# Halves of w_out and of two feed-forward units, made in the gate stage and fetched by DMA

## The chip, the cores and the metric

The kernel runs on one core of a Trainium2 chip. TensorE (PE) multiplies matrices; VectorE (DVE), ScalarE (ACT) and GpSimd (POOL) do elementwise work; SyncE (SP) issues DMA transfers, and ACT can issue them too, from its own instruction stream. The metric is the device time of one execution in microseconds (us). The two-letter names are those of the profile, where PEld is TensorE's weight load and SPq the DMA queue that SP issues to.

## The reference

One encoder layer on x of 1024 tokens by 1024 features, all in float32. Cut to what the kernel's stages around the change compute:

```python
q, k, v, r, lr_f, lr_b, u, g_a, g_b = split(rmsnorm(x) @ w_in)
o = gla(q, k, v, ...)                    # gated linear attention, both directions
y_a = (rmsnorm_head(o) * gla_norm * silu(r)) @ w_branch_gla
y_b = (multiscale_pool(u) @ w_pool_group) * pool_scale
merged = sigmoid(g_a) * y_a + sigmoid(g_b) * y_b
x = x + merged @ w_out
gate, up = split(rmsnorm(x) @ w_ffn_in)  # D_FF = 2816 each
x = x + (silu(gate) * up) @ w_ffn_out
return rmsnorm(x)
```

## The kernel before, in words

**Split operands.** Every float32 operand of a matmul is held as two parts in a narrower matmul type: hi is a cast on ACT (L172), lo is the operand less hi, a subtraction on DVE or POOL (L173). `products` (L250) makes three matmuls of them: hi by hi, hi by lo, lo by hi. The large products `o @ w_branch_gla`, `merged @ w_out` and the feed-forward ones are done with seven block products in place of eight (Strassen-like), so their operands are sums and differences of 512 x 512 blocks, numbered p = 1 to 7.

**Stages** (times by the profile's span): attention until some 405 us; the gate stage, 405 to 629; the branch product, 629 to 708; the out product with w_out, 708 to 813; the first feed-forward units, 813 to 900; the other units, and then the feed-forward output.

**The gate stage** is the loop `for g in range(GROUPS)`, with two feature blocks j for each g, so j runs from 0 to 7. Per j two weights `wa` and `wb` are multiplied (48 matmuls each, in two PSUM banks `ps`), and ACT evicts each bank with a sigmoid into `sa` (L899) and `sb` (L908). `take()` hands out a weight and begins the next, whose raw tiles SP loads (L180). `later` collects a store, and `flush` issues all that are collected, on SP (L686), at two places per j: behind the two halves of `wa` and behind those of `wb`. `weight_sums` runs beside this for j < 4, for w_branch_gla (two halves c of the rows) and then for w_out: it loads four raw blocks (`wsum`), POOL makes four sums or differences of 128 x 1024 in place (L750), and `later` stores them to `s_out` and `wt_out` in HBM. From j = 4 on, `beside` calls begin the data sums of the branch product.

**The branch and out products** share `project`: 14 pieces each (seven p, two halves c), 24 matmuls per piece. A piece needs data (`data_split`: ACT and DVE) and a weight (`weight_load` on SP into `wraw`, then `weight_split`: per half of 128 x 512 an ACT cast to `wh` and a POOL subtraction to `wl`). `line` lists the pieces; `line_make` makes the piece two ahead of the one that PE runs. The pool `wts` holds six buffers of `wh` and six of `wl`, shared with all other weights.

**Feed-forward units.** A `Unit` is one block of 128 gate and 128 up columns: two raw loads of 512 KB (`fraw`), up to four sums on DVE (`fs`, L1035), and seven `step`s, each with an ACT cast and a POOL subtraction of 128 x 512. Between the out product and the units, POOL makes the norm's scale (`n3rs`, L1150), DVE scales x to `xn` (L286), PE transposes `xn` (L1095) and ACT evicts it into `hb` (L1098), from which data halves `gh` and `gl` are split.

Tile's scheduler orders each engine's instructions; each engine runs its own list in order and waits on semaphores.

Of the kernel before, what the change touches and what calls it, by code (L numbers as in the profile page):

```python
# [3 lines left out]

# [6 lines left out]
F32 = mybir.dt.float32  # L11
# [6 lines left out]
P = 128  # L18
# [31 lines left out]
def kernel(  # L50
# [38 lines left out]
    def name(s):  # L89
        count[0] += 1  # L90
        return f"{s}_{count[0]}"

    def slot(dtype=F32, shape=(2, HALF), s="slot"):
        return slots.tile([P, *shape], dtype, tag="slot", name=name(s))
# [13 lines left out]
    def as_f32(ap):  # L108
        return ap.bitcast(F32)
# [61 lines left out]
    def split_to(hi, lo, src, eng=nc.vector):  # L171
        nc.scalar.copy(hi, src)  # L172
        eng.tensor_tensor(lo, src, as_f32(hi), op=ALU.subtract)  # L173
# [13 lines left out]
    class Weights:  # L187


        def __init__(self, tiles):  # L190
            self.per = tiles[0].shape[1]
            self.parts = []
            self.todo = [partial(self.split, raw) for raw in tiles]
            pending.extend(self.todo)
# [484 lines left out]
    deferred = []  # L679

    def later(dst, src):
        deferred.append(partial(nc.sync.dma_start, dst, src))

    def flush():
        while deferred:
# [42 lines left out]
    padd = partial(nc.gpsimd.tensor_tensor, op=ALU.add)  # L728


    s_out = {p: dram.tile([P, 4, HALF], F32, name=f"s_out{p}") for p in (3, 5, 6, 7)}
    wt_out = {p: dram.tile([P, 4, HALF], F32, name=f"wt_out{p}") for p in (4, 5, 6, 7)}

    def chunk(w, k_half, c_half, c):
        k0 = (4 * k_half + 2 * c) * P
        return w[k0 : k0 + 2 * P, c_half * HALF : (c_half + 1) * HALF].rearrange("(k p) c -> p k c", p=P)

    def weight_sums(w, c, left):
        raw = {}
        for i in range(2):  # L740
            for j in range(2):
                raw[i, j] = slot(s="wsum")
                nc.sync.dma_start(raw[i, j][:, :, :], chunk(w, j, i, c) if left else chunk(w, i, j, c))
        x11, x12, x21, x22 = (raw[i, j][:, :, :] for i in range(2) for j in range(2))
        if left:
            todo = [(padd, x22, x21, x22, 5), (psub, x21, x11, x21, 7), (psub, x11, x22, x11, 6), (psub, x12, x12, x11, 3)]
        else:
            todo = [(psub, x11, x12, x11, 5), (psub, x12, x22, x12, 7), (psub, x22, x22, x11, 6), (psub, x21, x21, x22, 4)]
        for op, dst, a, b, p in todo:
            op(dst, a, b)  # L750
            yield
            later((s_out if left else wt_out)[p][:, 2 * c : 2 * c + 2, :], dst)


    line, loads, made, begun_sums = [], [], [], []
# [18 lines left out]
    def weight_load(src):  # L774
        raw = slot(s="wraw")
        nc.sync.dma_start(raw[:, :, :], src)
        return raw

    def weight_split(raw):
        parts = []  # L780
        for k in range(2):
            hi = wts.tile([P, HALF], F32R, tag="wh", name=name("wh"))
            lo = wts.tile([P, HALF], F32R, tag="wl", name=name("wl"))
            split_to(hi[:, :], lo[:, :], raw[:, k, :], nc.gpsimd)
            parts.append((hi[:, :], lo[:, :]))
        return parts

    def data_split(src):
        hi, lo = slot(F32R, s="dh"), slot(F32R, s="dl")
        split_to(hi[:, :, :], lo[:, :, :], src[:, :, :])  # L790
        return [(hi[:, k, :], lo[:, k, :]) for k in range(2)]
# [39 lines left out]


    MERGED = (1, 7, 6, 5, 4, 2, 3)
    WEIGHT_B = {1: (0, 0), 2: (1, 0), 3: (1, 1)}
    merged = {}
    s3s = []

    def merged_piece(p, c):
        def load():
            if p in WEIGHT_B:  # L840
                return weight_load(chunk(w_out, *WEIGHT_B[p], c))
            return weight_load(wt_out[p][:, 2 * c : 2 * c + 2, :])

        def sums():
            def block(i, j):
                return merged[i, j][c][:, :, :]

            if p == 7:
                s3s.append(slot(s="s3"))
                sub(s3s[c][:, :, :], block(0, 0), block(1, 0))  # L850
            elif p == 6:
                padd(block(1, 0), block(1, 0), block(1, 1))
                sub(block(0, 0), block(1, 0), block(0, 0))
            elif p == 3:
                sub(block(0, 1), block(0, 1), block(0, 0))

        def make(raw):
            a = s3s[c] if p == 7 else merged[{1: (0, 0), 6: (0, 0), 5: (1, 0), 4: (1, 1), 2: (0, 1), 3: (0, 1)}[p]][c]
            return data_split(a), weight_split(raw)

        return load, sums, make

    line += [merged_piece(p, c) for p in MERGED for c in range(2)]

    sums_todo = [(w, c, left) for w, left in ((w_branch, True), (w_out, False)) for c in range(2)]
    summing = None
    def begin_first(c):
        begun[1, c] = data_split(ob[0, 0][c])

# [1 line left out]
    early += [partial(branch_sum, p, c) for p in (5, 7, 6) for c in range(2)]  # L871

    def beside(j):
        if j < 4:
            next(summing, None)
        elif early:
            early.pop(0)()

    for g in range(GROUPS):
        w = take()  # L880
        u = [t2(HALF + 2 * PAD, s="u") for _ in range(2)]
        nc.gpsimd.memset(u[0][:, :PAD], 0.0)
        nc.gpsimd.memset(u[1][:, PAD + HALF :], 0.0)
        for half in range(2):
            ps = feature_major(w, hT, half)
            nc.scalar.copy(u[half][:, PAD : PAD + HALF], ps[:, :])
        pool = slot(F32R, s="ph"), slot(F32R, s="pl")
        begin(pooled(g, u, *pool), 1)
        for j in (2 * g, 2 * g + 1):
            c = slice((j % 2) * P, (j % 2 + 1) * P)  # L890
            wa = take()
            if j == 2 * g:
                wp = take()(0)
            sa = slot(s="sa")
            if j < 4:
                summing = weight_sums(*sums_todo[j])
            for half in range(2):
                ps = feature_major(wa, hT, half)
                nc.scalar.activation(sa[:, half, :], ps[:, :], AF.Sigmoid)  # L899
                beside(j)  # L900
            flush()
            later(sa_out[:, :, j, :], sa[:, :, :])
            finish_side()
            wb = take()
            sb = slot(s="sb")
            for half in range(2):
                ps = feature_major(wb, hT, half)
                nc.scalar.activation(sb[:, half, :], ps[:, :], AF.Sigmoid)  # L908
                yb = bank(ps_g, "yb")
                mm3(yb[:, :], tuple(t[:, c] for t in wp), tuple(t[:, half, :] for t in pool), True, True)  # L910
                nc.vector.scalar_tensor_tensor(
                    sb[:, half, :], yb[:, :], g_pool[:, j : j + 1], sb[:, half, :], op0=ALU.mult, op1=ALU.mult
                )
                beside(j)
                if j == KT - 1 and half == 0:
                    line_make()
            if j < 4:
                next(summing, None)
            flush()
            later(yb_out[:, :, j, :], sb[:, :, :])  # L920
            if j == 3:
                for _ in range(3):
                    line_load()
            if j == KT - 1:
                line_make()
# [92 lines left out]
    class Unit:  # L1018
# [19 lines left out]
        def step(self, p=None):  # L1038

            if p is None:  # L1040
                if not self.todo:
                    return
                p = self.todo[0]
            self.todo.remove(p)
            if p in (5, 6) and not hasattr(self, "s1"):
                self.s1 = self.combined(self.block(1, 0), self.block(1, 1), ALU.add)
            if p == 1:
                src = self.block(0, 0)
            elif p == 6:
# [12 lines left out]
            lo = wts.tile([P, 4, P], F32R, tag="wl", name=name("wl"))[:, :, :]  # L1062
            split_to(hi, lo, src, nc.gpsimd)
            self.parts[p] = hi, lo
# [1 line left out]
        def __call__(self, p, k):  # L1066
            return tuple(t[:, k, :] for t in self.parts[p])

    f_order = [f for q in range(PAIRS) for f in (q, q + PAIRS)]
    units = []  # L1070

    def next_unit():
        if len(units) < FT:
            units.append(Unit(f_order[len(units)]))


    blocks, split_b, split_done = {}, {}, set()
# [470 lines left out]
```

## Time and profile before

| | |
|---|---|
| runs, median (lowest to highest of 3) | 1486.3 us (1485.8 to 1490.08) |
| profiled execution: time, span | 1487.58 us, 1485.8 us |
| mean granted clock of PE | 0.987 |
| instructions | 18520 |
| HBM read, written | 143.54 MB, 56.89 MB |

The profile shows one execution. It lists busy time per engine, the span in 40 slices, DMA queues, the chain that ended last, and the costliest groups of instructions: `out<-in`, shape, count, then busy time and mean length in ns, then the idle time ahead of them and what ended it. Other views answer for a stretch of the span: busy time by stage with the granted clock and DMA share, waits of an engine by the line and operation that released it, and the timeline.

### The profile page before, as it was taken

Reading aid. Unit: us, or ns where it says so; the run is one execution under the profiler, and the core shown is the slowest. Engines: PE = TensorE matmul, PEld = TensorE weight load, DVE = VectorE, ACT = ScalarE, POOL = GpSimd, SP = SyncE. Lnnn points to the kernel's source line nnn. Section 1 sums busy time; section 2 is a strip of 40 time slices with the busy share of each in tenths; the row PEclk is TensorE's granted clock in tenths of the full one; section 3 lists DMA queues with packets and bytes.
Section 4 is the critical chain, followed back from the end, with each engine's and each line's share of the span. In section 5 each row is a group of like instructions: output and inputs, shape, how many; then the busy total and the mean of one; then the engine's idle time right before and its main releaser. Section 6 shows DMA issues by size and latency. Waiting matters only on the chain. (4 is left out here: it accounts for less than half of the span.)

```text
span 1485.8 us, 18520 instructions
## 1 busy us (share of the span) xinstructions
PE 1419.6 (96%) x6797; PEld 1185.7 (80%) x6797; DVE 851.4 (57%) x1091; ACT 563.8 (38%) x1009; POOL 801.2 (54%) x544
## 2 busy tenths in 40 slices
PE   7999999999999999999888889999999999999988
PEld 7889898888888778878676667888888888787876
DVE  6175766761124053157783776677677777465375
ACT  6265555642122132244246533222333333443243
POOL 3241322312256432277897657667766668598345
PEclk9999999999999999999999989999999999999999
DMA  5120201001256732187242026444544456877352
GB/s 181 43 57 3 55 15 43 22 22 43 89 193 222 244 114 75 63 310 249 100 126 87 29 70 198 161 154 155 163 156 153 159 163 231 315 268 255 128 227 85
DMA packets 150523, 201.64 MB, mean 136 GB/s; under 512 B 9208, under 2 KB 96288, under 8 KB 150432
## 3 DMA queue, kind: packets, MB, share of 16 engines
q1 hardware_dynamic: 150432, 200.46, 40.4%
q8 instruction: 53, 0.87, 0.2%
q14 instruction: 38, 0.31, 0.1%
HBM read 143.54 MB, written 56.89 MB: 135 GB/s over the span
## 5 line engine op out<-in xcount | busy, mean ns | idle before, releaser
L173 POOL TENSOR_TENSOR wl<-raw,wh 128x512 fp32r<-128x512 f32 (+1 forms) x91 | 125.6, 1398 | 293.3 <-ACT wh L172 251.7
L250 PE MATMUL ps<-gh,wl 128*128 128x512 f32 x616 | 242.6, 394 | 9.4 <-POOL wl L173 9.4
L250 PE MATMUL ps<-gh,wh 128*128 128x512 f32 x616 | 243.0, 394 | 1.4 <-ACT wh L172 1.4
L250 PE MATMUL ps<-gl,wh 128*128 128x512 f32 x616 | 242.0, 393 | 0.0
L250 PE MATMUL ps<-hh,wh 128*128 128x512 f32 x576 | 228.5, 397 | 3.5 <-ACT wh L172 3.5
L250 PE MATMUL ps<-hh,wl 128*128 128x512 f32 x576 | 225.2, 391 | 0.6 <-POOL wl L173 0.6
L250 PE MATMUL ps<-hl,wh 128*128 128x512 f32 x576 | 225.0, 391 | 0.0
L173 POOL TENSOR_TENSOR wl<-fs,wh 128x512 fp32r<-128x512 f32 x88 | 127.7, 1453 | 107.0 <-ACT wh L172 75.8
L250 PEld LDWEIGHTS ps<-gh,wl 128*128 128x128 f32 x616 | 117.3, 190 | 35.7 <-POOL wl L173 11.0
L172 ACT CAST wh<-fs 128x512 fp32r<-128x512 f32 x88 | 54.6, 621 | 237.7 <-DVE fs L1035 237.7
L250 PEld LDWEIGHTS ps<-gh,wh 128*128 128x128 f32 x616 | 117.1, 190 | 26.0 <-ACT wh L172 2.3
L250 PEld LDWEIGHTS ps<-gl,wh 128*128 128x128 f32 x616 | 117.0, 190 | 24.0
L173 POOL TENSOR_TENSOR ol<-gor,oh 128x1024 fp32r<-128x1024 f32 (+1 forms) x42 | 108.8, 2607 | 47.6 <-ACT oh L172 35.2
L250 PEld LDWEIGHTS ps<-hh,wh 128*128 128x128 f32 x576 | 108.5, 188 | 25.1 <-ACT wh L172 3.9
L250 PEld LDWEIGHTS ps<-hh,wl 128*128 128x128 f32 x576 | 108.5, 188 | 24.2 <-POOL wl L173 1.1
L250 PEld LDWEIGHTS ps<-hl,wh 128*128 128x128 f32 x576 | 108.7, 189 | 21.0
L250 PE MATMUL ps<-oh,ol 128*128 128x512 f32 x308 | 120.2, 390 | 5.2 <-POOL ol L173 5.2
L250 PE MATMUL ps<-ol,oh 128*128 128x512 f32 x308 | 120.0, 390 | 2.9 <-DVE ol L173 2.9
L250 PE MATMUL ps<-oh,oh 128*128 128x512 f32 x308 | 120.0, 389 | 0.0
L173 POOL TENSOR_TENSOR wl<-wraw,wh 128x512 fp32r<-128x512 f32 x56 | 92.5, 1679 | 36.7 <-ACT wh L172 36.0
L173 DVE TENSOR_TENSOR ol<-wor,oh 128x1024 fp32r<-128x1024 f32 (+1 forms) x42 | 86.0, 2074 | 41.1 <-ACT oh L172 32.3
L173 POOL TENSOR_TENSOR wl<-fraw,wh 128x512 fp32r<-128x512 f32 x66 | 100.5, 1525 | 15.2 <-ACT wh L172 15.2
(246 smaller groups left out, 2894.7 us busy)
## 6 DMA issues: line engine op xcount, KB each, us to landing
raw<-in_w_in_dram SPq DMA_DIRECT2D x88, 256.0 KB, 3.3
fraw<-in_w_ffn_in_dram SPq DMA_DIRECT2D x44, 512.0 KB, 5.7
gor<-g_out SPq DMA_DIRECT2D x35, 512.0 KB, 5.2
g_out<-s SPq DMA_DIRECT2D x44, 256.0 KB, 2.4
wor<-t_out SPq DMA_DIRECT2D x20, 512.0 KB, 8.1
g_out<-g SPq DMA_DIRECT2D x33, 256.0 KB, 3.5
x<-in_x_dram SPq DMA_DIRECT2D x16, 512.0 KB, 4.4
wor<-in_w_ffn_out_dram SPq DMA_DIRECT2D x15, 512.0 KB, 7.5
```

The source lines that it names most:

```text
L172: nc.scalar.copy(hi, src)
L173: eng.tensor_tensor(lo, src, as_f32(hi), op=ALU.subtract)
L250: nc.tensor.matmul(ps, a[i], b[j], start=first and n == 0, stop=last and n == 2)
```

## The change

Four edits:

1. `later` issues its stores on ACT (`nc.scalar.dma_start`), all of them: `sa_out`, `yb_out`, `s_out`, and later `x2_out`.
2. For w_out, `output_parts` takes the place of `weight_sums`: all seven operands are made and split in the gate stage (hi on ACT, lo on DVE, 128 x 1024; the combinations stay on POOL), and both halves are stored to `wo_out`: 28 stores of 512 KB, where 8 sums were stored. In the out stage each piece fetches its four halves of 256 KB on SP straight into `wh` and `wl`; raw loads, casts and subtractions of these 14 pieces are gone.
3. `unit_parts` does the same for the first READY = 2 units: two loads, four combinations on POOL (128 x 512), seven casts on ACT, seven subtractions on DVE, seven stores of 512 KB each. A `ReadyUnit` step is two fetches of 256 KB.
4. Preparation is a chain of generators stepped four times per j through all eight j, so the early branch sums and `begin_first` move to j = 7 (two per step), and the first three loads of branch pieces from j = 3 to j = 6.

```diff
     def later(dst, src):
-        deferred.append(partial(nc.sync.dma_start, dst, src))
+        deferred.append(partial(nc.scalar.dma_start, dst, src))
...
+    def output_parts(c):
...
+        def parts(p, src):
+            hi, lo = slot(F32R, s="wph"), slot(F32R, s="wpl")
+            split_to(hi[:, :, :], lo[:, :, :], src)
+            for n, t in enumerate((hi, lo)):
+                later(wo_out[p][n][:, 2 * c : 2 * c + 2, :], as_f32(t[:, :, :]))
+
+        for p, src, dst, a, b in (
+            (1, b11, b11, b12, b11), (3, b22, b12, b22, b12), (7, b12, b22, b22, b11), (2, b21, b21, b21, b22)
+        ):
+            parts(p, src)
+            psub(dst, a, b)
+            if p in (3, 2):
+                yield
+        for p, src in ((5, b11), (6, b22), (4, b21)):
+            parts(p, src)
+            if p != 5:
+                yield
+        yield
+
+    def unit_parts(n):
...
+        def parts(p, src):
+            both = slot(F32R, s="up")
+            split_to(both[:, 0, :], both[:, 1, :], src)
+            later(u_out[n][p][:, :, :], as_f32(both[:, :, :]))
...
+        def weights():
+            parts = []
+            for k in range(2 * c, 2 * c + 2):
+                hi = wts.tile([P, HALF], F32R, tag="wh", name=name("wh"))
+                lo = wts.tile([P, HALF], F32R, tag="wl", name=name("wl"))
+                for n, t in enumerate((hi, lo)):
+                    nc.sync.dma_start(as_f32(t[:, :]), wo_out[p][n][:, k, :])
...
-            return data_split(a), weight_split(raw)
+            w = weights()
+            return data_split(a), w
...
+    preps = [g for c in range(2) for g in (branch_sums(c),)] + [output_parts(c) for c in range(2)]
+    preps = chain(*preps, *(unit_parts(n) for n in range(READY)))
...
     def beside(j):
-        if j < 4:
-            next(summing, None)
-        elif early:
-            early.pop(0)()
+        next(preps, None)
+        if j == KT - 1:
+            for _ in range(2):
+                early.pop(0)()
...
-            if j == 3:
+            if j == 6:
                 for _ in range(3):
                     line_load()
...
+    class ReadyUnit(Unit):
+        def step(self, p=None):
...
+            for i, t in enumerate((hi, lo)):
+                nc.sync.dma_start(as_f32(t), u_out[self.n][p][:, i, :].rearrange("p (k c) -> p k c", k=4))
```

The order of the matmuls on PE is the same. The other engines' lists change at these places. In the rows, the number behind a name is a counter; `wo_out_3987` to `wo_out_3993` are p = 1 to 7.

SP before, in the gate stage at j = 2 and 3: the stores of the sums stand between the loads of raw weights.

```order
L686 DMA yb_out<-sb_4319 256x1x512
L686 DMA wt_out_3988<-wsum_4529 128x1024
L180 DMA raw_4567<-in_w_in_dram 128x4x128
L180 DMA raw_4569<-in_w_in_dram 128x4x128
L686 DMA sa_out<-sa_4476 256x1x512
L686 DMA wt_out_3990<-wsum_4531 128x1024
L686 DMA wt_out_3989<-wsum_4535 128x1024
L686 DMA wt_out_3987<-wsum_4533 128x1024
L180 DMA raw_4648<-in_w_in_dram 128x4x128
L180 DMA raw_4650<-in_w_in_dram 128x4x128
```

ACT at the same place after: nine stores stand between the sigmoid of the second bank and the casts of the next weight; before, ACT went from the sigmoid straight to those casts.

```order
L172 CAST wph_4644<-wsum_4550 128x1024
L976 ACTIVATE sb_4599<-ps_4649 128x512
L172 CAST wph_4680<-wsum_4546 128x1024
L172 CAST wph_4684<-wsum_4552 128x1024
L686 DMA sa_out<-sa_4493 256x1x512
L686 DMA wo_out_3993<-wph_4639 128x1024
L686 DMA wo_out_3993<-wpl_4640 128x1024
L686 DMA wo_out_3988<-wph_4644 128x1024
...
L686 DMA wo_out_3992<-wpl_4685 128x1024
L172 CAST wh_4709<-raw_4697 128x512
L172 CAST wh_4719<-raw_4699 128x512
L967 ACTIVATE sa_4701<-ps_4702 128x512
```

POOL in the out stage before: the weights' low halves stand between the sums of merged blocks (L852) and the adds into x (L1179).

```order
L173 TENSOR_TENSOR wl_6356<-wraw_6309,wh_6355 128x512
L173 TENSOR_TENSOR wl_6360<-wraw_6309,wh_6359 128x512
L852 TENSOR_TENSOR mg_6046<-mg_6046,mg_6149 128x1024
L173 TENSOR_TENSOR wl_6408<-wraw_6349,wh_6407 128x512
L173 TENSOR_TENSOR wl_6412<-wraw_6349,wh_6411 128x512
L852 TENSOR_TENSOR mg_6047<-mg_6047,mg_6150 128x1024
L173 TENSOR_TENSOR wl_6448<-wraw_6401,wh_6447 128x512
L173 TENSOR_TENSOR wl_6452<-wraw_6401,wh_6451 128x512
```

After, POOL has there only the sums (L920), the adds (L1260, L1265) and the norm's scale (L1231), which now follows the adds directly.

```order
L920 TENSOR_TENSOR mg_6211<-mg_6211,mg_6312 128x1024
L920 TENSOR_TENSOR mg_6212<-mg_6212,mg_6313 128x1024
L1260 TENSOR_TENSOR x_1190_6348<-x_1190_6348,sum_6462 128x512
...
L1265 TENSOR_TENSOR x_1170_6249<-x_1170_6249,sum_6461 128x512
L1231 TENSOR_TENSOR n3rs_6893<-n3rs_6893,half_neg 128x1
L1231 TENSOR_TENSOR n3rs_6908<-n3rs_6908,half_neg 128x1
```

In its place SP has the fetches, four per piece, ahead of the out product:

```order
L1071 DMA x_1193_6354<-in_x_dram 128x1024
L908 DMA wh_6360<-wo_out_3987 128x512
L908 DMA wl_6361<-wo_out_3987 128x512
L908 DMA wh_6364<-wo_out_3987 128x512
L908 DMA wl_6365<-wo_out_3987 128x512
L908 DMA wh_6396<-wo_out_3987 128x512
```

More of the change, by code (lines that the diff above doesn't have):

```diff
@@ L2 @@
 from functools import partial
-from itertools import cycle
+from itertools import chain, cycle
 import concourse.bass as bass
@@ L731 @@
     s_out = {p: dram.tile([P, 4, HALF], F32, name=f"s_out{p}") for p in (3, 5, 6, 7)}
-    wt_out = {p: dram.tile([P, 4, HALF], F32, name=f"wt_out{p}") for p in (4, 5, 6, 7)}
+    wo_out = {p: dram.tile([2, P, 4, HALF], F32, name=f"wo_out{p}") for p in range(1, 8)}
+    READY = 2
+    f_order = [f for q in range(PAIRS) for f in (q, q + PAIRS)]
+    u_out = [{p: dram.tile([P, 2, HALF], F32, name=f"u_out{n}_{p}") for p in range(1, 8)} for n in range(READY)]
     def chunk(w, k_half, c_half, c):
@@ L736, in chunk, with branch_sums @@
         return w[k0 : k0 + 2 * P, c_half * HALF : (c_half + 1) * HALF].rearrange("(k p) c -> p k c", p=P)
-    def weight_sums(w, c, left):
+    def branch_sums(c):
         raw = {}
@@ L742, in weight_sums @@
                 raw[i, j] = slot(s="wsum")
-                nc.sync.dma_start(raw[i, j][:, :, :], chunk(w, j, i, c) if left else chunk(w, i, j, c))
+                nc.sync.dma_start(raw[i, j][:, :, :], chunk(w_branch, j, i, c))
+        yield
         x11, x12, x21, x22 = (raw[i, j][:, :, :] for i in range(2) for j in range(2))
[L745 to L748, printed above, removed]
@@ L749, in weight_sums @@
-        for op, dst, a, b, p in todo:
-            op(dst, a, b)
-            yield
-            later((s_out if left else wt_out)[p][:, 2 * c : 2 * c + 2, :], dst)
+        for op, dst, a, b, p in (
+            (padd, x22, x21, x22, 5), (psub, x21, x11, x21, 7), (psub, x11, x22, x11, 6), (psub, x12, x12, x11, 3)
+        ):
+            op(dst, a, b)
+            later(s_out[p][:, 2 * c : 2 * c + 2, :], dst)
+            if p in (7, 3):
+                yield
+        yield
+    def output_parts(c):
+        raw = {}
+        for i in range(2):
+            for j in range(2):
+                raw[i, j] = slot(s="wsum")
+                nc.sync.dma_start(raw[i, j][:, :, :], chunk(w_out, i, j, c))
+        yield
+        b11, b12, b21, b22 = (raw[i, j][:, :, :] for i in range(2) for j in range(2))
+        def parts(p, src):
[5 more added lines that the diff above has]
+            (1, b11, b11, b12, b11), (3, b22, b12, b22, b12), (7, b12, b22, b22, b11), (2, b21, b21, b21, b22)
+        ):
+            parts(p, src)
+            psub(dst, a, b)
+            if p in (3, 2):
+                yield
+        for p, src in ((5, b11), (6, b22), (4, b21)):
+            parts(p, src)
+            if p != 5:
+                yield
+        yield
@@ new lines, in unit_parts @@
+    def unit_parts(n):
+        raw = []
+        for c0 in (f_order[n] * P, D_FF + f_order[n] * P):
+            raw.append(slot(F32, (KT, P), "fraw"))
+            nc.sync.dma_start(raw[-1][:, :, :], w_ffn_in[:, c0 : c0 + P].rearrange("(k p) c -> p k c", p=P))
+        yield
+        a11, a12, a21, a22 = (t[:, 4 * j : 4 * j + 4, :].rearrange("p k c -> p (k c)") for t in raw for j in range(2))
+        def parts(p, src):
+            both = slot(F32R, s="up")
+            split_to(both[:, 0, :], both[:, 1, :], src)
+            later(u_out[n][p][:, :, :], as_f32(both[:, :, :]))
+        parts(1, a11)
+        parts(4, a22)
+        padd(a22, a21, a22)
+        psub(a21, a11, a21)
+        yield
+        parts(2, a12)
+        parts(5, a22)
+        psub(a11, a22, a11)
+        psub(a12, a12, a11)
+        yield
+        for p, src in ((7, a21), (6, a11), (3, a12)):
+            parts(p, src)
+        yield
+        yield
@@ L833 @@
     MERGED = (1, 7, 6, 5, 4, 2, 3)
-    WEIGHT_B = {1: (0, 0), 2: (1, 0), 3: (1, 1)}
     merged = {}
@@ L839, in load @@
         def load():
-            if p in WEIGHT_B:
-                return weight_load(chunk(w_out, *WEIGHT_B[p], c))
-            return weight_load(wt_out[p][:, 2 * c : 2 * c + 2, :])
+            return None
+        def weights():
[5 more added lines that the diff above has]
+                    nc.sync.dma_start(as_f32(t[:, :]), wo_out[p][n][:, k, :])
+                parts.append((hi[:, :], lo[:, :]))
+            return parts
         def sums():
@@ L858, in make @@
             a = s3s[c] if p == 7 else merged[{1: (0, 0), 6: (0, 0), 5: (1, 0), 4: (1, 1), 2: (0, 1), 3: (0, 1)}[p]][c]
-            return data_split(a), weight_split(raw)
+            w = weights()
+            return data_split(a), w
         return load, sums, make
     line += [merged_piece(p, c) for p in MERGED for c in range(2)]
-    sums_todo = [(w, c, left) for w, left in ((w_branch, True), (w_out, False)) for c in range(2)]
-    summing = None
+    preps = [g for c in range(2) for g in (branch_sums(c),)] + [output_parts(c) for c in range(2)]
+    preps = chain(*preps, *(unit_parts(n) for n in range(READY)))
     def begin_first(c):
@@ L894 @@
             sa = slot(s="sa")
-            if j < 4:
-                summing = weight_sums(*sums_todo[j])
             for half in range(2):
@@ L916 @@
                     line_make()
-            if j < 4:
-                next(summing, None)
             flush()
             later(yb_out[:, :, j, :], sb[:, :, :])
-            if j == 3:
+            if j == 6:
                 for _ in range(3):
@@ L1067, in __call__, with __init__ @@
             return tuple(t[:, k, :] for t in self.parts[p])
-    f_order = [f for q in range(PAIRS) for f in (q, q + PAIRS)]
+    class ReadyUnit(Unit):
+        def __init__(self, n):
+            self.n, self.parts, self.todo = n, {}, list(ORDER)
+        def step(self, p=None):
+            p = p or self.todo[0]
+            self.todo.remove(p)
+            hi = wts.tile([P, 4, P], F32R, tag="wh", name=name("wh"))[:, :, :]
+            lo = wts.tile([P, 4, P], F32R, tag="wl", name=name("wl"))[:, :, :]
+            for i, t in enumerate((hi, lo)):
+                nc.sync.dma_start(as_f32(t), u_out[self.n][p][:, i, :].rearrange("p (k c) -> p k c", k=4))
+            self.parts[p] = hi, lo
     units = []
@@ L1073, in next_unit @@
         if len(units) < FT:
-            units.append(Unit(f_order[len(units)]))
+            n = len(units)
+            units.append(ReadyUnit(n) if n < READY else Unit(f_order[n]))
     blocks, split_b, split_done = {}, {}, set()
```

## The prediction

> **What bounds the kernel now.** I read the page first, for the engine that fills the span.
>
> ```profile
> PE 1419.6 (96%) x6797; PEld 1185.7 (80%) x6797; DVE 851.4 (57%) x1091; ACT 563.8 (38%) x1009; POOL 801.2 (54%) x544
> PE   7999999999999999999888889999999999999988
> ```
>
> TensorE (PE) is busy for 96% of the span, and slices 20 to 24 of 40 (some 740 to 930 us) are the one dip after the start. The change leaves the list of matmuls alone, so it can only win PE's idle time and its time at a low clock. The second view gives busy time by stage: the stretch; its length, then PE, PEld, DVE, ACT, POOL; PE's granted clock, DMA share and GB/s.
>
> ```profile
> 461.00:517.00 56.00, 56.00 (x249) 46.39 (x248) 15.98 (x16) 11.75 (x22) 33.51 (x21) 1.00 0.70 231
> 517.00:573.00 56.00, 51.86 (x221) 42.13 (x220) 23.84 (x26) 15.48 (x27) 16.59 (x14) 0.97 0.41 122
> 400.00:629.00 229.00, 224.86 (x984) 185.44 (x983) 68.76 (x76) 52.67 (x94) 97.28 (x64) 0.99 0.48 154
> 629.00:708.00 79.00, 76.77 (x335) 62.27 (x334) 53.91 (x51) 32.45 (x48) 57.25 (x38) 1.00 0.73 266
> 708.00:813.00 105.00, 90.67 (x369) 69.12 (x368) 71.61 (x76) 47.31 (x84) 91.85 (x54) 0.93 0.33 108
> 813.00:900.00 87.00, 72.05 (x297) 57.00 (x296) 64.15 (x67) 35.23 (x54) 52.75 (x33) 0.90 0.23 76
> 900.00:1000.00 100.00, 100.00 (x442) 82.52 (x441) 67.97 (x77) 29.74 (x52) 72.72 (x51) 1.00 0.48 158
> ```
>
> In this order: the four-weight part of the gate stage in which sums of weights are made, what follows it, the whole gate stage, the branch products, the out stage, the first feed-forward units, and the steady state. The gate stage has room on every engine. The out stage has POOL at 91.85 of 105 us, and PE idle for 14.33 us; the first units have 14.95 us idle. The clock there is 0.93 and 0.90: (1 - 0.93) x 105 = 7.4 us and (1 - 0.90) x 87 = 8.7 us more. Lost in both: 29.3 + 16.1 = 45.4 us. From 900 on nothing is lost at first, so most of what can be won lies here. The third view, PE's waits (total, times, longest), out stage first, then first units:
>
> ```profile
> PE ps L250 <- POOL wl L173: 8.8, 9, 2.9
> PE ps L250 <- ACT hb L1098: 1.8, 2, 1.6
> PE tr L1095 <- DVE xn L286: 1.3, 1, 1.3
> PE ps L250 <- ACT wh L172: 0.4, 1, 0.4
> ...
> PE ps L250 <- POOL wl L173: 9.4, 3, 3.9
> PE tr L1095 <- DVE xn L286: 2.2, 1, 2.2
> PE tr L1095 <- ACT hb L1098: 1.8, 1, 1.8
> PE ps L250 <- ACT wh L172: 1.4, 1, 1.4
> ```
>
> Of 29.3 us idle, 8.8 + 0.4 + 9.4 + 1.4 = 20.0 wait for a half of a weight, nearly all for the low half that POOL subtracts. That low clocks follow such waits is in the timeline (start, length, idle before):
>
> ```profile
> 777.43 0.39 PE L250 MATMUL ps<-wh,dl 128*128 128x512 f32 x1
> 777.66 0.39 PE L250 MATMUL ps<-wh,dh 128*128 128x512 f32 x1
> 779.89 0.50 PE L250 MATMUL ps<-wl,dh 128*128 128x512 f32 x1 [1.84 <-POOL wl L173]
> 782.57 0.63 PE L250 MATMUL ps<-wl,dh 128*128 128x512 f32 x1
> 783.00 0.63 PE L250 MATMUL ps<-wh,dl 128*128 128x512 f32 x1
> 898.04 0.50 PE L250 MATMUL ps<-gh,wl 128*128 128x512 f32 x1 [2.96 <-POOL wl L173]
> ...
> 779.90:784.00 4.10, 4.10 (x10) 2.89 (x11) 0.00 (x0) 0.83 (x4) 4.10 (x4) 0.58 0.40 161
> 868.40:872.40 4.00, 3.94 (x9) 3.17 (x10) 4.00 (x5) 1.24 (x2) 4.00 (x4) 0.50 0.59 172
> 898.00:902.00 4.00, 3.96 (x16) 3.03 (x17) 0.54 (x1) 1.11 (x2) 4.00 (x3) 1.00 0.70 214
> ```
>
> Matmuls start 0.23 us apart before the wait of 1.84 us and 0.43 apart after it, at a clock of 0.58 for 4.1 us; the longest wait, of 3.9, is followed by 0.50; one of 2.96 by no drop. So a wait of 2 to 4 us costs its length again, mostly, and I let the clock loss go with the waits.
>
> **The change, out stage and first units.** Removed from POOL: 28 subtractions for w_out, half of the first row, and 14 for two units.
>
> ```profile
> L173 POOL TENSOR_TENSOR wl<-wraw,wh 128x512 fp32r<-128x512 f32 x56 | 92.5, 1679 | 36.7 <-ACT wh L172 36.0
> 778.57 4.97 POOL L173 TENSOR_TENSOR wl<-wraw,wh 128x512 fp32r<-128x512 f32 x4
> 784.09 0.76 DVE L286 TENSOR_SCALAR xn<-x,n3rs 128x1024 f32<-128x1024 f32 x1 [4.34 <-POOL n3rs L1150]
> L173 POOL TENSOR_TENSOR wl<-fraw,wh 128x512 fp32r<-128x512 f32 x66 | 100.5, 1525 | 15.2 <-ACT wh L172 15.2
> L172 ACT CAST wh<-fs 128x512 fp32r<-128x512 f32 x88 | 54.6, 621 | 237.7 <-DVE fs L1035 237.7
> ```
>
> That is 28 x 1.68 = 47 us of POOL's work for the out stage and 14 x 1.53 = 21 for the units; from ACT 42 x 0.62 = 26 us of casts; DVE loses its 8 sums for the units, some 10 us (128x512, taken at 1.25 us, between half and the whole of the 1.63 that a 128x1024 subtraction takes in a row below). The weight waits go: 20.0 less the 2.96 at 898, which stands at a unit beyond the two, gives 17. The third row shows who else stood behind POOL: four subtractions in a row until 783.5, then n3rs (the norm's scale), then DVE's xn, then PE's transposes. Of 1.3 + 2.2 us for xn I take 3 away, of 1.8 + 1.8 for hb (ACT, with fewer casts in its queue) 2. With the waits 22 of 29.3 us idle go, and of the 16.1 us at low clock the share of the longer waits, some 13. Together -35.
>
> What is late next: PE's wish for data that DVE splits (dl, gl). DVE has 136 of 192 us busy in these stages, less some 10 for the sums gone, in a time that shrinks to 159: 0.79, with adds into the merge and the residual that come in bursts. And the fetches: 56 + 28 of 256 KB on SP, issued two pieces ahead, into buffers that PE frees only one piece before. A piece is 24 matmuls of 0.227 = 5.4 us, so they have 5 to 10 us.
>
> ```profile
> raw<-in_w_in_dram SPq DMA_DIRECT2D x88, 256.0 KB, 3.3
> wraw<-s_out SPq DMA_DIRECT2D x8, 512.0 KB, 8.5
> ```
>
> The same size lands in 3.3 us where DMA is half free, and 512 KB in 8.5 us in the branch stage at a share of 0.73. Four of them are 1 MB per piece: 193 GB/s, below the 266 that the branch stage carried. Mostly in time; I give back 2 for fetches and DVE. Out stage and units: -33; with half of it back under other names -18; with all 45.4 gone but the 2.96 at 898 and half of hb's waits -40. I stay nearer the second, since the waits named POOL are the most of the row.
>
> **The gate stage.** Here two bad things before: PE waited once for 3.5 us, and its clock cost 0.03 x 56 = 1.7.
>
> ```profile
> 522.66 0.50 PE L250 MATMUL ps<-hh,wh 128*128 128x512 f32 x1 [3.52 <-ACT wh L172]
> 509.36 2.79 SPq L686 DMA_DIRECT2D wt_out<-wsum  x2
> 514.13 1.62 SPq L180 DMA_DIRECT2D raw<-in_w_in_dram  x2
> ```
>
> SP's stores of the sums wait for POOL, and the next raw weights stand behind them on SP. On ACT's queue the stores no longer hold a load: -5.8 (4.14 idle, 1.7 clock) at best. New work here, by rows:
>
> ```profile
> L172 ACT CAST dh<-o x12: 1038/1048/1052, 531.8 to 696.0; 128x1024 fp32r<-128x1024 f32 x12
> L173 DVE TENSOR_TENSOR dl<-o,dh x12: 1210/1628/2334, 534.2 to 697.0; 128x1024 fp32r<-128x1024 f32 x12
> L686 SPq DMA_DIRECT2D s_out<-wsum x8: 319/339/560, 414.3 to 454.7; - x8
> 418.80 8.49 SPq L686 DMA_DIRECT2D s_out<-wsum  x3
> ```
>
> ACT: 14 x 1.05 + 14 x 0.62 = 23.4 us of casts and 66 stores at 0.34, 22 us, atop 52.67 of 229. DVE: 14 x 1.63 + 14 x 0.8 (half the size) = 34 atop 68.76. POOL: 8 combinations of half size, about 10 atop 97.28; its full-size combinations stay as many. All far below the stage's length, so the sums themselves are hidden by PE's 225 us. What is not hidden is order: ACT drains PSUM (two sigmoids per weight, three banks, each filled in 5.4 us), and a flush of nine stores holds it for 9 x 0.34 = 3.1 us, longer if a store waits for its data. The last row is what that looks like on SP: 8.49 us for three stores, waiting for POOL's sums. Since a flush stands behind the second sigmoid, ACT then has 5.4 us until the next bank is full and a spare bank after that. Bytes: +14.7 (w_out's parts) + 7.3 (units) - 4.2 (old sums) + 2.1 (units' raw) = +20 MB on 229 us x 154 GB/s = 35, so 241 GB/s on average. In the middle, where both kinds of load and store meet, some 25 MB fall in 70 us: 357 GB/s, against 231/0.70 = 330 at a full share. So the tail of that is late by about 5 us at the stores, which nothing needs soon, but raw loads share it. I take -5.8 + 2 = -4; bounds -5.8, and +14 if the raw loads starve for a weight and a half.
>
> **Branch stage.** The first pieces are loaded at the seventh weight and not at the fourth, six branch sums move to the last weight: +1 (-2 to +4; 2.23 us idle there now).
>
> **Sum.** -33 - 4 + 1 = -36 on the profiled execution's 1487.6, which is 1.3 above the median of the runs: 1451.6 and 1450.3. Rounded against myself, since each removed wait was priced with its clock, 1453. Ends: -40 - 5.8 - 2 is 1440; -18 + 0 + 4 is 1473.
>
> **The rivals.** A, the forecast, 1440 to 1465. A2, the same, but the low clock of the out stage isn't its waits' doing (0.58 after 1.84 us, 1.00 after 2.96): its 7.4 us stay, and 1453 + 7 = 1460. The longest weight wait there is 2.9, against 3.9 in the first units. The Trainium skill's "TensorE: Matmul & The Clock Gate", Part 1, would have it so: the clock is halved only after an idle window of about 3.4 us. The trace's 2.96 agrees with that, its 1.84 doesn't. B, the waits come back on other names: DVE's low halves or late fetches keep half of the 33: 1487.6 - 16.5 - 4 + 1 = 1468. For it: DVE at 0.79 in bursts, buffers freed late; against: at 900 to 1000 DVE runs 0.68 with PE at 100.00 of 100. C, the gate stage runs out of DMA: 25 MB at 330 GB/s take 76 us, and if the raw loads wait their turn in it, PE loses two or three times 5 us with the clock's share: +15 instead of -4, 1471. For it: the 357 against 330. Against: raw weights are fetched a weight (10.9 us) ahead. The Trainium skill's "DMA: Bandwidth & Descriptors", section "Issuing engines are not separate DMA queues", speaks for C: putting stores on ACT saves only issue time, since all queues run on the same 16 engines; no row of before has two queues, so the trace can't say. D, slower: ACT, held by stores that wait for sums or splits, drains PSUM late. 16 flushes (two per weight), each holding PE for 2 us with as much again at low clock, are 16 x 4.2 = 67, less 33: 1521. It decides from 36 / 16 = 2.3 us lost per flush. For it: the 8.49 us; against: ACT comes to the stores late, when POOL and DVE, both under half busy, have run ahead. E, no change (1482 to 1491): the waits for POOL turn whole into waits for DVE or the fetches, and the flushes cost what the 3.5 us wait gave; nothing in the rows is that large.
>
> **How the numbers follow.** A 0.52, A2 0.10, B 0.18, C 0.08, D 0.08, E 0.04. The range leaves out 1 in 10 at the top (D and part of E) and a little below: 1440 to 1474. A change of 0.3% (4.5 us) is about what a measurement can tell: faster A + A2 + B + C = 0.88, same 0.04, slower 0.08.
>
> **What would show it.** Right: no PE wait for POOL wl between 700 and 860, the clock of those stages at 0.97 or more, PE idle below 10 us there; POOL's busy time near 45 in the out stage; no 3.5 us wait at 522. B: new waits on DVE dl, gl or on DMA wh, wl. C: waits on ACT wh <- DMA raw at 460 to 560 with the DMA share at 1.0. D: PE waits on ACT sa or sb at each flush. Wrong would be the forecast if the low clock stays without the waits, or the gate stage grows past 240 us.

## The result, and the profile after

The changed kernel takes 1452.8 us (median of 5, 1452.43 to 1456.13), 0.9775 (95% interval 0.9759 to 0.9791) of the time before, which was 1486.8 us in five runs: 34 us less. Its profiled execution took 1452.8 us with a span of 1451.1, against 1487.58 and 1485.8, so 34.7 us went from the span. They are best split at the first matmul of each stage, since the matmuls are the same. The view of busy time by stage, of the changed kernel (columns as in the prediction): gate, branch, out, and the first units up to 860, where the view stops just short of the end of a wait that is told of below.

```profile
395.11:632.98 237.87, 231.46 (x1003) 190.07 (x1002) 99.05 (x101) 73.42 (x121) 114.13 (x74) 0.99 0.71 241
632.98:709.54 76.56, 76.45 (x337) 62.99 (x336) 58.59 (x53) 31.49 (x45) 58.34 (x38) 1.00 0.72 256
709.54:794.19 84.65, 81.43 (x370) 65.95 (x368) 63.84 (x76) 32.48 (x57) 38.28 (x24) 1.00 0.66 204
794.19:860.00 65.81, 62.50 (x287) 50.31 (x285) 51.50 (x58) 27.30 (x40) 28.75 (x18) 1.00 0.52 182
```

The out stage is 84.65 us long where it was 105.12, with 3.2 us of PE idle and the clock at 1.00; POOL is busy there for 38 us where it was 92. The gate stage is 4.4 us longer than its 233.46 before. The out stage and the units are best compared over the same 655 matmuls, from the out product's first to the one that waits at 898.04 before and at 862.35 now; the kernel before first:

```profile
708.27:898.04 189.77, 160.49 (x655) 124.32 (x653) 135.00 (x143) 82.54 (x138) 142.37 (x85) 0.92 0.28 91
709.54:862.35 152.81, 143.92 (x655) 116.25 (x654) 117.00 (x135) 61.44 (x100) 69.38 (x43) 1.00 0.61 196
```

They take 37.0 us less: PE's idle time falls from 29.3 to 8.9 us, and the busy time of the same matmuls by 16.6, as their clock rises from 0.92 to 1.00. PE's waits, gate stage first, then 700 to 800, then 800 to 870:

```profile
PE ps L250 <- ACT wh L172: 5.2, 2, 2.8
PE ps L250 <- POOL wl L173: 1.2, 2, 0.6
...
PE ps L250 <- DVE dl L173: 2.4, 2, 1.5
PE tr L1176 <- ACT hb L1179: 0.7, 1, 0.7
...
PE ps L250 <- POOL wl L173: 4.0, 2, 3.8
PE tr L1176 <- ACT hb L1179: 1.4, 1, 1.4
PE tr L1176 <- DVE xn L286: 0.2, 1, 0.2
```

Every wait for a weight of w_out or of the two units is gone; what is left of POOL's, 3.8 us at 862, is a unit's that is not made ahead (the fourth's, as the last experiments show). It is the matmul that waited 2.96 us at 898 before; now it waits longer, and slow clock follows it. The change took three things off these stages at once, raw loads, casts and subtractions; PE's waits name the subtractions, and most of POOL's idle time ahead of those ended with ACT's casts (36.0 of 36.7 us in the prediction's row); no run removes one of the three alone. The branch stage has no wait at all. The two waits of the gate stage are new. One of them in PE's timeline, and ahead of it ACT's, where ACTq rows are the issues of stores from ACT's instruction stream:

```profile
498.69 0.50 PE L250 MATMUL ps<-hh,wh 128*128 128x512 f32 x1 [2.75 <-ACT wh L172]
...
488.37 0.54 ACTq L686 DMA_DIRECT2D sa_out<-sa  x1
488.95 0.62 ACTq L686 DMA_DIRECT2D wo_out<-wph  x1
490.49 1.22 ACTq L686 DMA_DIRECT2D wo_out<-wph  x1
...
496.83 1.15 ACTq L686 DMA_DIRECT2D wo_out<-wpl  x1
498.02 0.62 ACT L172 CAST wh<-raw 128x512 fp32r<-128x512 f32 x1 [8.60 <-issue]
```

The row of nine stores lasts from 488.37 to 498.0 us. From the fourth store on an issue takes some 1.2 us. The cast of the next weight's high half stands behind them, PE behind the cast, and POOL's low half (0.62 us more) behind it too. From the fourth store on the DMA engines are full, at a share of 1.03:

```profile
490.50:498.00 7.50, 5.43 (x24) 4.15 (x23) 2.25 (x1) 0.00 (x0) 1.17 (x1) 1.00 1.03 407
```

### The profile page after: what moved, and what is told of

It reads as the page before. It is cut to its first block, busy times and chain, and to the rows that moved or that the text cites. A ratio compares the mean times of both kernels' runs of the same rounds, so it can differ in the third digit from the quotient of the medians.

```text
span 1451.1 us, 18652 instructions
## 1 busy us (share of the span) xinstructions
PE 1405.5 (97%) x6797; PEld 1179.6 (81%) x6797; DVE 872.5 (60%) x1111; ACT 561.8 (39%) x995; POOL 743.8 (51%) x510
## 5 line engine op out<-in xcount | busy, mean ns | idle before, releaser
L173 POOL TENSOR_TENSOR wl<-fs,wh 128x512 fp32r<-128x512 f32 x80 | 112.4, 1405 | 97.9 <-ACT wh L172 69.7
L172 ACT CAST wh<-fs 128x512 fp32r<-128x512 f32 x80 | 49.8, 622 | 230.2 <-DVE fs L1101 221.4
L173 POOL TENSOR_TENSOR wl<-fraw,wh 128x512 fp32r<-128x512 f32 x60 | 94.3, 1571 | 16.3 <-ACT wh L172 16.3
L250 PE MATMUL ps<-wh,hh 128*128 128x256 f32 x256 | 79.7, 311 | 0.0
```

The source lines that it names most:

```text
L250: nc.tensor.matmul(ps, a[i], b[j], start=first and n == 0, stop=last and n == 2)
```

## The experiments

All runs stand against the kernel before, which ran beside them (1486.8 to 1488.2 us). "Time" is the median of the runs; the lengths of the stages are those of one profiled execution, in us; "rest" is from the first unit's first matmul to the end of the span.

| kernel | time | gate | branch | out | rest |
|---|---|---|---|---|---|
| before | 1486.8 | 233.46 | 79.61 | 105.12 | 672.4 |
| changed | 1452.8 | 237.87 | 76.56 | 84.65 | 656.9 |
| act_alone | 1480.4 | 226.90 | 76.56 | 106.40 | 673.9 |
| wout_only | 1477.2 | 235.84 | 76.56 | 92.17 | 672.3 |
| units_only | 1462.5 | 225.53 | 76.61 | 105.15 | 658.6 |
| sp_queue | 1479.6 | 258.21 | 79.75 | 84.62 | 660.5 |
| spread3 | 1442.8 | 225.54 | 76.56 | 84.68 | 657.1 |
| halves | 1458.5 | 240.80 | 76.62 | 84.62 | 659.1 |
| ready3 | 1480.0 | 261.91 | 76.55 | 84.66 | 660.3 |
| ready3_spread3 | 1469.8 | 251.30 | 76.56 | 85.00 | 660.1 |
| wout_spread3 | 1464.9 | 225.53 | 76.59 | 91.05 | 675.8 |
| spread3_third_dve | 1446.3 | 227.59 | 76.56 | 84.67 | 660.6 |
| spread3_fourth_dve | 1442.5 | 225.53 | 76.56 | 84.66 | 659.3 |

### The parts, one at a time

**The queue alone** (act_alone), the kernel before with

```diff
     def later(dst, src):
-        deferred.append(partial(nc.sync.dma_start, dst, src))
+        deferred.append(partial(nc.scalar.dma_start, dst, src))
```

> The kernel before with the stores of `later` on ACT's queue, nothing else. If the gain comes from the weight halves that no longer wait for POOL, this gives only what the raw load held behind a store cost in the gate stage: the 3.5 us wait at 522 and its slow clock, -4 to -6 us, 1481 to 1483. If freeing SP's queue is a large part of the gain (the loads of branch, out and unit weights also stand on SP), it gives -10 or more, 1476 or less. If stores on ACT hold up evictions at once, it is slower than 1487.

Measured: 1480.44 us, 0.9945 (0.9934 to 0.9957), -7.75 us. Its gate and branch stages by the view of busy time by stage:

```profile
395.23:622.13 226.90, 226.90 (x1002) 187.87 (x1001) 67.54 (x75) 53.17 (x93) 99.71 (x66) 1.00 0.54 172
622.13:698.69 76.56, 76.45 (x338) 62.99 (x336) 53.67 (x51) 33.59 (x49) 56.36 (x38) 1.00 0.69 236
```

PE is busy for the whole of the gate stage: -6.6 us, as the 3.52 us wait, the 0.62 behind it and the clock had promised. The branch stage loses its three waits as well (-3.05), which no theory had, and so the time is just below the first range, and far from the 1476 of the second. The queue alone does it. A likely way is in SP's list, before first and then with the queue alone:

```profile
629.70 0.51 SPq L686 DMA_DIRECT2D yb_out<-sb  x1
630.32 1.43 SPq L965 DMA_DIRECT2D gate<-sa_out  x2
...
601.64 9.91 SPq L965 DMA_DIRECT2D gate<-sa_out  x2
```

Before, the loads of `gate` tiles for the merge stand behind a store and begin 1.7 us after the stage's first matmul (628.66); with the queue alone they begin 20 us ahead of it (622.13). That this is what removes the waits was not tested by itself.

**w_out's halves alone** (wout_only) and **the ready units alone** (units_only):

```diff
-    READY = 2
+    READY = 0
```

and, for the other, w_out as before:

```diff
-            w = weights()
-            return data_split(a), w
+            return data_split(a), weight_split(raw)      # raw: from w_out or wt_out, as before
...
-        def parts(p, src): ...                           # in output_parts
+        for dst, a, b, p in ((x11, x12, x11, 5), (x12, x22, x12, 7), (x22, x22, x11, 6), (x21, x21, x22, 4)):
+            psub(dst, a, b)
+            yield
+            later(wt_out[p][:, 2 * c : 2 * c + 2, :], dst)
```

> The changed kernel with READY = 0: w_out's halves are made ahead, the first units are as before. If the two parts act each in its own stage, the out stage keeps its -20 and the branch stage its -3, the gate stage its +4 (its two rows of nine stores are w_out's), and the units keep their waits for POOL (two, 2.5 and 3.9 us, with slow clock): 1466 to 1470. Rival: the units' waits were a backlog that POOL brought out of the out stage, so they go too: 1453 to 1458.

> The changed kernel with w_out as before (eight sums stored, raw weights loaded and split on ACT and POOL in the out stage); the two units ready. If the parts act each in its own stage: gate -6, branch -1 to -3, out stage 0 to -3, units -16: 1461 to 1465. Rival: the first units' trouble comes from the out stage (x, n3rs, xn and hb late behind POOL), and ready units alone give little: 1472 to 1480.

Measured: 1477.15 us, 0.9923 (0.9911 to 0.9935), and 1462.46, 0.983 (0.9817 to 0.9843). The units by themselves came as expected, at the size the theory of separate stages gives: rest -13.8, or -15.3 against the queue alone. w_out by itself came out 7 us above the upper end of the theory of separate stages, and further from the rival. Against the queue alone its out stage gains 14.2 us and the gate stage loses 8.9. By the medians only some 3 us are left; the profiled execution, at 1473.85 us the fastest of the five, shows 7. In that out stage, PE's waits include one that the full change does not have, for a fetched half:

```profile
766.88 0.47 PE L250 MATMUL ps<-wh,dh 128*128 128x512 f32 x1 [1.68 <-DMA wh<-wo_out]
395.20:631.04 235.84, 229.37 (x996) 188.47 (x995) 85.96 (x87) 66.20 (x107) 101.18 (x65) 0.99 0.62 208
707.60:799.77 92.17, 85.53 (x369) 67.69 (x368) 64.07 (x76) 34.24 (x60) 41.34 (x27) 0.96 0.65 193
```

The rows below it are its gate and out stages. So the two parts help each other: with ready units too the out stage is 7.5 us shorter again (84.65), with 3.2 us idle in place of 6.6 and the clock at 1.00 in place of 0.96. Together, by the medians, from the queue alone (1480.4): -3.3 for w_out, -18.0 for the units, -27.6 for both.

### Where the gate stage's loss comes from

**The stores back on SP** (sp_queue):

```diff
-        deferred.append(partial(nc.scalar.dma_start, dst, src))
+        deferred.append(partial(nc.sync.dma_start, dst, src))
```

> The changed kernel with the stores back on SP. If ACT, which took 1.2 us for each of nine stores in a row, is what holds PE twice in the gate stage (2.75 + 0.62 and 2.41 + 0.62 us, and slow clock behind them), these two waits go, and if nothing else takes their place it is some 10 us faster, 1443. Rival: the stores now stand ahead of raw weight loads on SP and wait there for POOL's, ACT's and DVE's work, so raw loads come late for several weights: 1465 to 1490.

Measured: 1479.64 us, 0.9941 (0.9927 to 0.9955). The rival holds. PE's waits in the gate stage, and SP's timeline ahead of the longest of them:

```profile
PE ps L250 <- ACT wh L172: 17.4, 6, 6.6
...
496.32 0.32 SPq L686 DMA_DIRECT2D wo_out<-wpl  x1
496.73 0.38 SPq L686 DMA_DIRECT2D wo_out<-wph  x1
499.94 0.32 SPq L686 DMA_DIRECT2D wo_out<-wpl  x1
500.35 0.39 SPq L686 DMA_DIRECT2D wo_out<-wph  x1
501.07 0.49 SPq L686 DMA_DIRECT2D wo_out<-wpl  x1
501.66 2.50 SPq L180 DMA_DIRECT2D raw<-in_w_in_dram  x2
```

Here an issue takes 0.3 to 0.5 us, yet stores stand 3 us apart, each low half waiting for DVE's subtraction; the raw weight is loaded behind the last of them. Without ACT's queue, 27 of the 34 us are lost again.

**At most three stores behind each half** (spread3): four places per j instead of two rows of any length.

```diff
-    def flush():
-        while deferred:
+    def flush(most=99):
+        for _ in range(min(most, len(deferred))):
             deferred.pop(0)()
...
                 beside(j)
-            flush()
+                flush(3)        # inside the loop over the halves, of wa and of wb
```

> The changed kernel with at most three stores issued behind each half of a weight (four places per j instead of two rows of any length). If the row of nine stores on ACT (10 us long, since an issue takes 1.2 us once some stores are under way) is what holds PE in the gate stage, the waits of 2.75 + 0.62 and 2.41 + 0.62 us and the slow clock behind them (0.16 x 11 + 0.14 x 12 = 3.4 us) go: 1442 to 1446. Rival: the DMA engines are full there, and raw loads or ACT's issues wait in other places: 1450 to 1456.

Measured: 1442.79 us, 0.97 (0.9683 to 0.9717), 10 us less than the change; of all kernels here only a variant of it, told of last, is as fast. The gate stage, and the issues of high halves (minimum, median, maximum in ns), of this kernel and then of the changed one:

```profile
395.22:620.76 225.54, 225.54 (x997) 186.81 (x995) 99.70 (x101) 73.82 (x121) 115.68 (x73) 1.00 0.76 258
...
L686 ACTq DMA_DIRECT2D wo_out<-wph x14: 326/508/1305, 473.0 to 542.4; - x14
...
L686 ACTq DMA_DIRECT2D wo_out<-wph x14: 326/944/1223, 474.4 to 552.0; - x14
```

PE never idles in 225.54 us, with all the added casts and subtractions in it and 22 MB more moved than before (225.54 us at 258 GB/s, against 233.46 at 154). So neither the work nor the bytes cost anything in themselves; the rows did.

**The price of an issue** (halves): each store of w_out's parts as two of 256 KB.

```diff
-                later(wo_out[p][n][:, 2 * c : 2 * c + 2, :], as_f32(t[:, :, :]))
+                for k in range(2):
+                    later(wo_out[p][n][:, 2 * c + k, :], as_f32(t[:, k, :]))
```

> The changed kernel with each store of 512 KB of w_out's parts issued as two of 256 KB. If an issue under load costs 1.2 us whatever its size, the rows of nine become 17 issues of 1.2 us, 20 us, and PE is held some 10 us longer at two places: 1470 or more. If the time is that of the bytes before it in the queue, an issue takes 0.6 us and the rows stay as long: 1451 to 1458.

Measured: 1458.45 us, 0.9806 (0.979 to 0.9821).

```profile
L686 ACTq DMA_DIRECT2D wo_out<-wph x28: 326/594/848, 472.9 to 556.2; - x28
489.04 1.28 ACTq L686 DMA_DIRECT2D wo_out<-wpl  x2
PE ps L250 <- ACT wh L172: 9.5, 2, 4.9
```

In the row an issue takes half as long, two together 1.28 us where one of 512 KB took 1.15 to 1.22. It goes by bytes, about 512 KB per 1.2 us, or 430 GB/s, which is near the 407 GB/s that the full DMA engines moved in the changed kernel's row. There is a little on top for the count, which lengthened the two waits: from 489 to 498 us the engines moved 349 GB/s here, at a share of 1.07. 1458.5 is half a us beyond what the theory of bytes allowed, and far from 1470.

**w_out alone without rows** (wout_spread3): `flush(3)` as above and READY = 0.

> w_out's halves alone (READY = 0) with at most three stores behind each half of a weight. If the small gain of w_out's part by itself (3 us beyond the queue's own) is a gain of 14 us in the out stage less 9 us lost in the gate stage at the rows of nine stores, the gate stage comes back to some 226 us and the whole to 1464 to 1469. If the gate stage loses that time to the added bytes and not to the rows, it stays at 1474 to 1479.

Measured: 1464.88 us, 0.9849 (0.9833 to 0.9866). The gate stage is back at 225.53: by the medians the rows alone had hidden 12 us of w_out's gain, and 10.3 of them are seen in the gate stage of the two profiles.

### The weight wait that is left

**READY = 3** (ready3), and the same with at most three stores (ready3_spread3):

```diff
-    READY = 2
+    READY = 3
...
         next(preps, None)
+        if j in (4, 5):
+            next(preps, None)
...
         def step(self, p=None):          # of ReadyUnit
+            if p is None and not self.todo:
+                return
```

> The changed kernel with READY = 3 (two more steps of preparation in each half of j = 4 and 5, so that all fits). The last large weight wait of the first units (3.79 us at 862, with a slow clock behind it) belongs to the third unit. If it goes: -4 to -6, 1447 to 1449. Rival: the seven more stores and the doubled steps hold ACT in the gate stage for as much: 1451 to 1458. Or the wait moves to the fourth unit: no change.

> READY = 3 and at most three stores behind each half of a weight. If both act by themselves: 1437 to 1442. If the third unit only moves its wait to the fourth: as the kernel with at most three stores alone, 1442 to 1446.

Measured: 1479.99 us, 0.9951 (0.9936 to 0.9967), and 1469.78, 0.988 (0.9864 to 0.9895). Both expectations missed by far, in the gate stage and beyond it. Of the first kernel, PE's two longest waits in the gate stage, its longest wait behind it, and ACT ahead of the first of them:

```profile
583.54 0.79 PE L250 MATMUL ps<-hh,wh 128*128 128x512 f32 x1 [12.40 <-ACT wh L172]
558.00 0.80 PE L250 MATMUL ps<-hh,wh 128*128 128x512 f32 x1 [10.28 <-ACT wh L172]
...
884.32 0.77 PE L250 MATMUL ps<-gh,wh 128*128 128x512 f32 x1 [6.40 <-DMA wh<-u_out]
...
565.74 0.62 ACT L172 CAST up<-fraw 128x512 fp32r<-128x512 f32 x1 [6.27 <-DMA fraw<-in_w_ffn_in_dram]
...
571.87 0.62 ACT L172 CAST up<-fraw 128x512 fp32r<-128x512 f32 x1 [1.05 <-POOL fraw L807]
573.54 0.62 ACT L172 CAST up<-fraw 128x512 fp32r<-128x512 f32 x1 [1.05 <-POOL fraw L808]
574.11 8.73 ACTq L686 DMA_DIRECT2D u_out<-up  x7
582.87 1.14 ACT L172 CAST wh<-raw 128x512 fp32r<-128x512 f32 x2 [8.72 <-issue]
```

ACT first waits 6.27 us for a unit's raw block, then steps with POOL from combination to combination, then issues a row of eight stores, and only then casts the weight for which PE waits 12.4 us. I put that down to the doubled steps, which leave less time between a unit's loads and its casts; no run has the third unit without them. The third unit itself gains nothing either: PE waits 6.40 us for one of its fetches, which SP issued behind the raw loads of the next unit. With three stores at most the rows go but not ACT's waits for raw blocks and for POOL, and the gate stage is still 26 us longer than without the third unit. A third unit prepared at the old pace was not tried.

**The third unit's low halves on DVE** (spread3_third_dve), on the kernel with at most three stores, and then **of the fourth unit the first weight's low half alone** (spread3_fourth_dve):

```diff
+            self.lo = nc.vector if len(units) == READY else nc.gpsimd      # the third unit
...
-            split_to(hi, lo, src, nc.gpsimd)
+            split_to(hi, lo, src, self.lo)
```

```diff
+            self.at = len(units)
...
-            split_to(hi, lo, src, nc.gpsimd)
+            split_to(hi, lo, src, nc.vector if self.at == 3 and p == 1 else nc.gpsimd)
```

> At most three stores behind each half of a weight, and the low halves of the third unit's weights subtracted on DVE instead of POOL. If the 3.79 us wait at 850 is POOL's order (the low half stands behind an operation on wot that waits 4.29 us for a DMA), it goes, with the slow clock behind it: 1436 to 1440. Rival: DVE, which holds g and sums for PE's banks there, is late instead: 1441 to 1446.

> At most three stores behind each half of a weight, and of the fourth unit the first weight's low half alone subtracted on DVE instead of POOL. Moving the third unit's halves left POOL idle for 25 us and PE's wait in place; the low half in question is the fourth unit's first, behind an operation on wot that waits for a DMA. If that order is the cause, the 3.79 us wait shrinks to below 1.5, with the slow clock behind it: 1437 to 1441. Rival: the raw weights of the fourth unit, loaded just behind wot's, come late themselves, and the wait stays under another name (DVE wl): 1441 to 1446.

Measured: 1446.3 us, 0.9724 (0.9705 to 0.9743), and 1442.51, 0.9698 (0.9676 to 0.972): some 3.5 us more than the kernel with at most three stores, though the two intervals overlap, and the same as it. Neither fell below the rivals' ranges. PE's wait in that kernel and POOL ahead of it, then the same with the third unit's halves on DVE, then with the fourth unit's first:

```profile
850.47 0.79 PE L250 MATMUL ps<-gh,wl 128*128 128x512 f32 x1 [3.79 <-POOL wl L173]
847.90 1.29 POOL L1380 TENSOR_TENSOR wot<-wot 128x512 f32<-128x512 f32 x1 [4.29 <-DMA wot<-in_w_ffn_out_dram]
849.15 1.27 POOL L173 TENSOR_TENSOR wl<-fraw,wh 128x512 fp32r<-128x512 f32 x1
...
856.17 0.80 PE L250 MATMUL ps<-gh,wl 128*128 128x512 f32 x1 [4.91 <-POOL wl L173]
853.18 1.26 POOL L1381 TENSOR_TENSOR wot<-wot 128x512 f32<-128x512 f32 x1 [25.12 <-DMA wot<-in_w_ffn_out_dram]
...
852.05 0.50 PE L250 MATMUL ps<-gh,wl 128*128 128x512 f32 x1 [2.77 <-POOL wl L173]
850.73 1.26 POOL L173 TENSOR_TENSOR wl<-fs,wh 128x512 fp32r<-128x512 f32 x1
```

With the third unit off POOL, POOL idles for 25 us and the wait is there all the same: my name for it was wrong, it is not the third unit's. It is the fourth unit's first weight, whose low half stands on POOL behind an operation that waits for wot's DMA. Taken off POOL, it hands the wait on to the same unit's second weight, 1.6 us later and 1.0 us shorter. Nothing measurable is won, and the rivals' own reasons (DVE late, raw weights late) are not what the waits name either.

## Why the prediction was right, and where it was not

The time, 1452.8, is what was forecast, but of the sum's three terms none is right by itself: -33, -4 and +1 were forecast, -36.0 (-20.5 in the out stage, -15.5 in the rest), +4.4 and -3.05 were measured. The first two lie inside their stated bounds, the third does not. The errors cancel, and that is luck.

**Out stage and first units.** The mechanism is as forecast: the waits for POOL's low halves go, and with them xn's (3.5 to 0.2 us) and part of hb's (4.7 before, with one of 1.0 that the forecast's rows leave out; 2.0 now). The 2 us given back for fetches and DVE are about right: the waits for dl rise from 0.6 to 2.4 us, and no fetch is waited for. Over the same 655 matmuls 20.4 us of idle time went, where 22 less these 2 were counted on. POOL's 38 us of work in the out stage are near the 45 named. Low clock went whole over these matmuls (16.6 us), where 13 were counted on. Behind them the wait at 862, kept at its 2.96 us in the forecast and now 3.79 long, costs 0.39 x 4 = 1.6 us of slow clock, where before none followed it. So 20.4 + 16.6 - 1.6 = 35.4 of the 36.0 us are accounted for, and the clock is most of the 3 us by which this term was too small. A2 is out: the clock of the out stage is 1.00 once its waits are gone.

**What a wait costs in clock** stays unsettled. Two waits of the changed kernel, of 2.75 and 3.79 us, are followed by

```profile
498.69:502.70 4.01, 3.38 (x9) 2.36 (x10) 1.69 (x1) 2.40 (x4) 2.52 (x2) 0.70 0.92 257
862.40:866.40 4.00, 4.00 (x11) 3.19 (x12) 0.44 (x1) 0.00 (x0) 4.00 (x3) 0.61 0.65 203
```

and the one of 1.54 us by no drop that shows in its stage. The rule of the Trainium skill's "TensorE: Matmul & The Clock Gate", Part 1, an idle window of about 3.4 us, agrees with the second; the first, like the 1.84 us of before, comes below it. Behind the first stands one more wait of 0.62 us, and the slow matmuls begin only after that one. In the timelines of all 13 kernels, from 390 to 1000 us, each of the 22 waits of PE above 2.97 us is followed by matmuls of 0.63 us in place of 0.39. Of the shorter ones some are (1.84 us at 779.89 before) and others not (2.96 us at 898.04 before). What decides between these is open.

**Gate stage.** This is the step that failed: "a flush of nine stores holds it for 9 x 0.34 = 3.1 us". The row of before from which 0.34 came shows stores that SP issued one to three at a time. In a row the issues took 0.5 to 0.8 and then 1.2 us, as the DMA engines were full (1.03 at 407 GB/s), so the flush held ACT for 9.6, more than the 5.4 and a spare bank that were to cover it. And what stood behind it was not the eviction of a bank, as the text had it, but the casts of the next weight. The forecast's rival D had the mechanism and missed the number: 2 of 16 flushes hold PE, for 3.4 and 3.0 us, with slow clock behind; together 12.3 us of stage, by the kernel with three stores at most. D's condition, 2.3 us on each of 16 flushes, was far off. At 237.87 us the stage came near the 240 that the text had named as a sign of being wrong. The gain of the queue was forecast well: -5.8 against -6.6.

**Rival C** had its condition and not its effect. DMA was full for stretches, but no raw load held PE for it: the kernel with three stores at most moves the same bytes in a stage with no PE idle at all, through stretches as full as this one:

```profile
500.00:510.00 10.00, 10.00 (x46) 8.29 (x45) 2.73 (x3) 2.05 (x3) 2.01 (x2) 1.00 1.04 367
```

The price that full engines did take is that of the rows, by way of ACT. Of C's two figures the 25 MB were too many (20 MB in the changed kernel from 490 to 560 us, 285 GB/s) and the 330 GB/s too low (407). The rule named for it is in the Trainium skill's "DMA: Bandwidth & Descriptors", section "Issuing engines are not separate DMA queues". It says that a second queue saves only the issuing time, usually small. The runs differ: here the queue was worth 7.75 us by itself and 27 us with the halves, through order: on SP a store that waits for its data holds up the raw weights behind it.

**Branch stage.** +1 was forecast for the moved loads and sums, and -3.05 came. With the queue alone the same 76.56 us come out, so beside the queue's gain the moves cost nothing that shows.

**Rival B** didn't come about: DVE runs 64 of 84.65 us in the out stage, 0.75, and PE waits for it for 2.4 us in all.

## What to carry to other kernels

Work that is moved to where an engine has room costs nothing there as work; it costs where it stands in an engine's list. Before adding stores to a compute engine's stream, count how many stand in a row ahead of an instruction that the bound engine waits for, and price each by its bytes under load and not by a lone issue: at most three at a time cost nothing here, two rows of nine 12.3 us. And check a forecast by its stages: a sum that is right can be two errors.

## What the runs showed of the hardware

The time an engine spends on issuing a DMA isn't fixed. On ACT it was 0.33 us for a store of 512 KB alone, 1.15 to 1.22 from the fourth in a row on, and 0.6 for 256 KB in such a row. In a row it follows the bytes, at some 430 GB/s, where the DMA engines were full at 407; a store of 512 KB in 256 rows (`yb_out`, right behind the nine) took 1.18 us, no longer than one in 128. In the row of nine the casts behind it start only when the last issue has ended, as the 8.60 us of idle time named "issue" show. But ACT's work and its issues can overlap: the cast that began at 488.37, 1.05 us long, ran beside the row's first two issues.
